# Neighbourhood attention with a stationary split V and a feature-major output, and later q/k weights split in the V stage

## The chip, the cores and the metric

One core of a Trainium2 chip runs the whole program. The metric is device time in microseconds, from runs of the complete kernel. The core has five instruction streams: TensorE (PE, matmuls, with its weight loads as PEld), VectorE (DVE), ScalarE (ACT), GpSimd (POOL) and SyncE (SP, which issues most of the loads). Each stream runs its instructions in order; they wait for each other by semaphores. SBUF is the working memory with 128 partitions, PSUM is where TensorE writes.

## The reference

One encoder layer in float32 over 1280 tokens (256 of a prompt, 1024 of a sample), model width 1024:

```
proj = rmsnorm(x) @ w_in            # columns: latents for group A | q, k, v for group B
a = mla_group(...)                  # 8 heads, dense attention over low-rank latents
b = na_group(...)                   # 8 heads of 64, 2-D neighbourhood attention
mix = concat(rmsnorm(a) * g_a, rmsnorm(b) * g_b)
x = x + mix @ w_o
x = x + (silu(h2 @ w_gate) * (h2 @ w_up)) @ w_down      # h2 = rmsnorm(x)
y = rmsnorm(x)
```

In group B each token attends to a window of at most 8 rows x 16 columns of a grid 64 wide, with a learned bias:

```
s = where(col_mask, q_row @ k_band.T + bias, -1e30)
p = softmax(s)
o = p @ v_band
```

## The kernel before

Tokens are reordered on the host so that a window falls into few tiles of 128 tokens: a query tile of the sample (tiles 2 to 9) needs its own key tile and its two neighbours, the two of the prompt (tiles 0 and 1) need each other. Products that must keep float32 accuracy are made in the type F32R: an operand is split into a high and a low part, and `mm3` (L108) issues three matmuls, high by high, high by low and low by high.

The stages follow each other. The first makes the normalised input, kept transposed as `hT_h` and `hT_l`, and the latents of group A. Then come q and k of the first pair of heads (`qk_weights`, L325, and `qk_ftile`, L336). `qk_weights` loads a raw 128-column weight, scales and splits it on GpSimd (L331, L333 through L94 and L96) into `wqk_h` and `wqk_l`, each with two buffers. `qk_ftile` projects it in three chunks of tokens into the PSUM tile `pj` and evicts it.

The V stage (L380 to L398) loads eight raw V weights into eight buffers, splits them on ScalarE and VectorE (`split_g`, L133), and for each of ten token tiles makes 24 matmuls into a bank of the two-bank PSUM tile `na_t`. One copy on ScalarE (L397) puts the result into `V`, in plain float32, which stays in SBUF for all heads.

The neighbourhood attention runs over four pairs of heads (L529). `na_bias(p)` (L414) loads and adds up the bias of the pair on GpSimd. `na_pair(p, ...)` (L455) takes ten query tiles, and in each of them two heads. For one head of one query tile:

- a copy of the query part on GpSimd (`qz`, L485), two score matmuls (L486, L487)
- bias and row extreme on VectorE (L497), exponential and row sum on ScalarE (L500)
- a transpose of each key tile's probabilities on TensorE (L504) into `na_t`, evicted by ScalarE for the first head (L507) and by VectorE for the second (L509)
- the product with V (L512): the transposed probabilities are stationary, 64 columns of `V` move, in plain float32. Each such call appears in the trace as two matmuls.

Then the query tile is divided by its row sums on VectorE (L517, L519) and stored token-major to `b_d`. While one pair attends, the projections of the next pair's q and k are what else TensorE has; the last pair has none, but some first projections of the latent attention (`project_first`, L665), held behind units of the last pair by `held`.

After the latent attention (L743) the output stage takes token tiles in turn. `mix_in` (L863) loads both groups' halves, makes their sums of squares and scales each half by its own factor on GpSimd (L877); `mix_T` (L882) transposes the eight 128-column blocks on TensorE and splits them; `out_proj` (L897) makes 24 matmuls for each half of the output into one PSUM bank and adds the residual on VectorE (L907). The FFN follows.

The order on SP's queue is the order of the program. On the other engines a planner orders the instructions at build time by its own estimate of their times, with earlier code preferred; `tc.issue_after(x)` puts an instruction behind `x` on its engine. A pool's tile with `bufs=n` has n slots: a new use of a slot waits until the former one is finished. Pools are stacked from both ends of SBUF, and a pool that is allocated where another was released waits tile by tile.

Of the kernel before, what the change touches and what calls it, by code (L numbers as in the profile page):

```python
# [11 lines left out]
F32 = mybir.dt.float32  # L12
# [6 lines left out]
P = 128  # L19
# [9 lines left out]
DH = 64  # L29
# [10 lines left out]
def encoder_trunk(ctx: ExitStack, tc: tile.TileContext, x_tm, x_T, g_attn, w_c, w_v, w_qk,  # L40
# [8 lines left out]
    b_d = tc.dram_tile([NTOK, 512], F32, name="b_d")  # L49
# [22 lines left out]
    def store_r(out, in_):  # L72
        nc.scalar.dma_start(out=out.bitcast(F32), in_=in_.bitcast(F32))

# [44 lines left out]
    rb = pool("rb", side="right")  # L119
    ra = pool("ra", side="right")  # L120
# [18 lines left out]
    def load_wc(kc):  # L139
        nm = {0: "wqk_raw", 1: "wqk_h", 2: "wqk_l", 3: "wqk_h", 4: "wqk_l", 7: "wqk_raw"}.get(kc)  # L140
        raw = (rb.tile([P, KC, P], F32, name=nm, bufs=1 if nm == "wqk_raw" else 2)
# [104 lines left out]
    def load_wr():  # L246
        raw = (rb.tile([P, KC, P], F32, name="wqk_raw").rearrange("p a b -> p (a b)")
               [:, 0:768].rearrange("p (c n) -> p c n", c=3))
        load(raw, w_qr)
        split_w(wr[:, 0], wr[:, 1], raw)  # L250
# [74 lines left out]
    def qk_weights(i):  # L325
        raw = rb.tile([P, KC, P], F32, name="wqk_raw")
        load(raw, w_qk[i])
        wh = rb.tile([P, KC, P], F32R, name="wqk_h", bufs=2)
        wl = rb.tile([P, KC, P], F32R, name="wqk_l", bufs=2)
        for ks in (slice(0, 4), slice(4, 8)):  # L330
            nc.gpsimd.tensor_tensor(out=raw[:, ks], in0=raw[:, ks], op=ALU.mult,  # L331
                                    in1=ga[:, ks].unsqueeze(2).to_broadcast([P, 4, P]))
            step["qkw"] = split_w(wh[:, ks], wl[:, ks], raw[:, ks])  # L333
        wqk[i] = wh, wl

    def qk_ftile(i, chunks=CHUNKS):  # L336
        wh, wl = wqk[i]
        dst = rq if (i // 2) % 2 == 0 else rc
        nm = "qk"[i % 2]
        if i not in qk:  # L340
            qk[i] = ([dst.tile([P, NTOK], F32R, name=f"{nm}{x}") for x in "ab"] +
                     [dst.tile([P, NTOK], F32R, name="kl") if nm == "k" else None])
        ab, kl = qk[i][0:2], qk[i][2]
# [32 lines left out]
    ra.release()  # L376
    pa.release()
# [3 lines left out]
    V = rV.tile([P, NT, 512], F32, name="V")  # L381
    rv = pool("rv", side="right")
    wv = []
    for kc in range(KC):
        raw = rv.tile([P, 512], F32, name="wv_raw", bufs=8)
        load(raw, w_v[kc])
        h = rv.tile([P, 512], F32R, name=f"wv_h{kc}")
        l = rv.tile([P, 512], F32R, name=f"wv_l{kc}")
        step["wv", kc] = split_g(h, l, raw, kc)
        wv.append((h, l))  # L390
    for t in range(NT):
        ts_ = slice(t * P, (t + 1) * P)
        pv = pb.tile([P, 512], F32, name="na_t", bufs=2)
        for kc in range(KC):
            mm3(pv, hT_h[:, kc, ts_], hT_l[:, kc, ts_], wv[kc][0], wv[kc][1],
                kc == 0, kc == KC - 1)
        nc.scalar.copy(out=V[:, t], in_=pv)  # L397
    rv.release()  # L398
    qk_ftile(1, CHUNKS[1:])


    rc = pool("rc", side="right")
    rcm = pool("rcm", side="right")
# [1054 lines left out]
```

## Time and profile before

| | |
|---|---|
| runs of the kernel | 1612.18, 1613.79, 1613.88 us (median 1613.79) |
| profiled execution, its span | 1610.3 us (the page gives no other time of it) |
| granted TensorE clock, mean | 0.998 |
| TensorE busy | 1582.5 us, 98% of the span |
| VectorE, ScalarE, GpSimd busy | 893.3, 717.2, 666.1 us |
| V stage | 137 to 193 us |
| neighbourhood attention | 193 to 381 us |
| latent attention | 381 to 663 us |
| output stage | 663 to 791 us |

The span is the time from the first to the last instruction on the profiled core. "Busy" is time in which an engine had an instruction running; matmuls overlap one another, so the duration of one matmul is longer than the step from its start to the next one's. An "x" is a count; `<-` in brackets names what ended the idle time before an instruction.

### The profile page before, as it was taken

How to read it: one execution, taken by the hardware profiler on the slowest of the kernel's cores; microseconds unless marked ns; L12 is line 12 of the kernel's file. 1: busy time of each engine (PE TensorE's matmuls, PEld its weight loads, DVE VectorE, ACT ScalarE, POOL GpSimd, SP SyncE). 2: the span in 40 equal slices, each digit the busy share in tenths (PEclk: the TensorE clock that was granted, in tenths of full speed). 3: DMA queues.
4: the chain of work that ended last, by engine and by line, in shares of the span. 5: the costliest groups of instructions: out<-in, count | busy, mean ns of one | idle time of the engine just before them, and what ended most of it. 6: DMA issues, size and time to landing. Idle time of an engine off the chain costs nothing.

```text
span 1610.3 us, 25767 instructions
## 1 busy us (share of the span) xinstructions
PE 1582.5 (98%) x9616; PEld 1443.1 (90%) x9616; DVE 893.3 (55%) x1501; ACT 717.2 (45%) x1492; POOL 666.1 (41%) x833
## 2 busy tenths in 40 slices
PE   8999999999999999999999999999999999999998
PEld 8998789998888888888899999999999998888886
DVE  5853045566677777443583444334444246886676
ACT  6533144465777777544453323233222332443334
POOL 4633235544211129224676665565666651010002
PEclk9999999999999999999999999999999999999999
DMA  8626022152100030234312232222232237843534
GB/s 294 202 70 160 19 53 63 37 209 62 32 20 26 24 119 20 80 118 144 125 67 65 89 110 97 71 87 89 97 110 76 70 128 269 296 140 96 157 103 155
DMA packets 121772, 171.09 MB, mean 106 GB/s; under 512 B 35376, under 2 KB 65840, under 8 KB 121648
## 3 DMA queue, kind: packets, MB, share of 16 engines
q1 hardware_dynamic: 78880, 120.30, 24.3%
q10 hardware_dynamic: 41952, 46.08, 8.2%
q0 software_dynamic: 816, 3.08, 0.5%
q8 instruction: 75, 1.23, 0.3%
q14 instruction: 49, 0.40, 0.1%
HBM read 118.96 MB, written 50.46 MB: 105 GB/s over the span
## 4 chain that ended last, share of the span: by engine, by line
PE 90%; POOL 3%; ACT 2%; DVE 2%; DMA 1%; issue 1%; SPq 0%; ACTq 0%; POOLq 0%; DVEq 0%
PE M L112 11%; PE M L110 10%; PE M L111 10%; PE d L111 5%; PE d L110 5%; PE d L112 5%; PE o L788 4%; PE tp L778 4%; PE na_o L512 3%; PE po L110 2%; PE pj L110 2%; PE pj L111 2%; PE pj L112 2%; PE po L111 2%; PE po L112 2%; PE S L110 2%
## 5 line engine op out<-in xcount | busy, mean ns | idle before, releaser
L111 PE MATMUL M<-S,wc 128*128 128x320 f32 x1056 | 323.8, 308 | 0.0
L110 PE MATMUL M<-S,wc 128*128 128x320 f32 x1056 | 321.3, 309 | 2.5 <-ACT S L962 1.2
L112 PE MATMUL M<-S,wc 128*128 128x320 f32 x1056 | 312.0, 309 | 2.4 <-POOL wc L970 2.4
L110 PEld LDWEIGHTS M<-S,wc 128*128 128x128 f32 x1056 | 197.3, 188 | 3.7 <-ACT S L962 1.5
L111 PEld LDWEIGHTS M<-S,wc 128*128 128x128 f32 x1056 | 198.2, 188 | 0.0
L112 PEld LDWEIGHTS M<-S,wc 128*128 128x128 f32 x1056 | 194.7, 188 | 3.0 <-POOL wc L970 3.0
L970 POOL TENSOR_TENSOR wc<-A,wc 128x512 fp32r<-128x512 f32 x86 | 121.1, 1409 | 81.6 <-ACT wc L969 81.5
L1052 DVE TENSOR_TENSOR z<-M,z 128x320 f32<-128x320 f32 x120 | 57.2, 487 | 129.6 <-PE M L112 109.1
L969 ACT CAST wc<-A 128x512 fp32r<-128x512 f32 x86 | 53.5, 622 | 158.4 <-PE M L111 148.8
L970 POOL TENSOR_TENSOR wc<-sum,wc 128x512 fp32r<-128x512 f32 x62 | 88.5, 1427 | 85.8 <-ACT wc L969 85.7
L1052 DVE TENSOR_TENSOR zB<-M,zB 128x320 f32<-128x320 f32 x100 | 47.6, 488 | 133.4 <-PE M L112 109.9
L111 PE MATMUL d<-S,S 128*128 128x512 f32 (+1 forms) x314 | 121.1, 386 | 0.0
L112 PE MATMUL d<-S,S 128*128 128x512 f32 (+1 forms) x314 | 120.7, 386 | 0.0
L110 PE MATMUL d<-S,S 128*128 128x512 f32 (+1 forms) x314 | 120.4, 387 | 0.0
L100 DVE TENSOR_TENSOR PT<-tp,PT 128x512 fp32r<-128x512 f32 (+1 forms) x144 | 93.2, 658 | 33.9 <-ACT PT L99 32.7
L969 ACT CAST wc<-sum 128x512 fp32r<-128x512 f32 x62 | 38.4, 619 | 144.0 <-PE M L111 99.6
L99 ACT CAST PT<-tp 128x512 fp32r<-128x512 f32 (+1 forms) x144 | 79.2, 567 | 33.5 <-PE tp L778 30.2
L770 DVE TENSOR_REDUCE mm<-S 128x1 f32<-128x1024 f32 (+1 forms) x80 | 85.0, 1062 | 13.5 <-PE S L112 11.9
L1099 ACT CAST S<-as 128x640 fp32r<-128x640 f32 x58 | 42.2, 728 | 105.7 <-issue 62.7
L772 ACT ACTIVATE ex<-S,mm 128x1024 f32<-128x1024 f32 (+1 forms) x80 | 79.7, 997 | 14.9 <-DVE mm L770 13.6
L801 POOL TENSOR_TENSOR ob<-ob 128x128 f32<-128x128 f32 x40 | 18.5, 461 | 160.8 <-ACT ob L798 157.3
L788 PE MATMUL o<-PT,v 128*128 128x256 f32 x544 | 80.4, 287 | 0.9 <-ACT PT L99 0.9
(432 smaller groups left out, 4115.8 us busy)
## 6 DMA issues: line engine op xcount, KB each, us to landing
as<-act_d SPq DMA_DIRECT2D x73, 320.0 KB
w<-in_w_down_dram SPq DMA_DIRECT2D x44, 256.0 KB
act_d<-z ACTq DMA_DIRECT2D x35, 320.0 KB
act_d<-zB ACTq DMA_DIRECT2D x35, 320.0 KB
A<-in_w_gate_dram SPq DMA_DIRECT2D x42, 256.0 KB
A<-in_w_up_dram SPq DMA_DIRECT2D x42, 256.0 KB
x<-in_x_tm_dram SPq DMA_DIRECT2D x20, 512.0 KB
cT_d<-stg ACTq DMA_DIRECT2D x20, 320.0 KB
```

The lines of the kernel that those rows point to most:

```text
L99: i = nc.scalar.copy(out=hi, in_=ps)
L100: nc.vector.tensor_sub(out=lo, in0=ps, in1=hi)
L110: nc.tensor.matmul(out, lhsT=sh, rhs=mh, start=first, stop=False, **kw)
L111: nc.tensor.matmul(out, lhsT=sh, rhs=ml, start=False, stop=False, **kw)
L112: return nc.tensor.matmul(out, lhsT=sl, rhs=mh, start=False, stop=last, **kw).ins
L770: nc.vector.reduce_max(out=nm[:, u:u + 1], in_=S, axis=AX.X, negate=True)
L772: nc.scalar.activation(ex, S, AF.Exp, bias=nm[:, u:u + 1], scale=1.0, accum_out=l[:, u:u + 1])
L778: nc.tensor.transpose(tp[:, j], ex[:, kt * P:(kt + 1) * P], ident)
L788: nc.tensor.matmul(oT, lhsT=vv, rhs=pt[s][g][:, j], start=kt == 0 and s == 0, stop=kt == nkt - 1 and s == 1)
L969: i0 = nc.scalar.copy(out=hi, in_=raw)
L970: i1 = nc.gpsimd.tensor_tensor(out=lo, in0=raw, in1=hi, op=ALU.subtract)
L1052: nc.vector.tensor_add(out=o, in0=ps, in1=a)
```

## The change

It touches five places.

1. **V.** The evicted V of each token tile is split into high and low parts, `[head][part][64]`, by ScalarE and VectorE (`split_ps`). The first pair's stays in SBUF, as five tiles of two token tiles each (`na_values`); the other three pairs' are stored to DRAM (`vn_d`) from GpSimd's queue and read back by SP, three tiles ahead of a pair and two within it (`bring`). The raw V weights have four buffers in place of eight.
2. **Product with V.** `na_pair` takes query tiles two at a time. Each head's exponentials are multiplied by the reciprocal of their sum on GpSimd before the transposes, the transposed tile is evicted as a high part by ScalarE and a low part by VectorE, and the product has the 128 columns of split V stationary. The moving operand is the high and then the low part of the probabilities: 256 columns for a key tile that both query tiles need, 128 for one that only one needs. The two 64-row halves of the result are added (one copy on ScalarE, one addition on VectorE for each head), and the result is stored feature-major to `bT_d`.
3. **Weights.** The q and k weights of pairs 1 to 3 are loaded, scaled and split in the V stage by ScalarE and VectorE (`later_weights`, twelve half-weights in four pieces each), stored to `wqk_d` from ScalarE's queue, and read back by SP as `wqk_h` and `wqk_l`. The split on GpSimd is left for pair 0 only. In program order, the weights of pairs 2 and 3 are fetched before the preceding pair attends.
4. **Bias.** A pair's sample bias is made after the pair before it, in one buffer (`na_bias`); the prompt's in two steps (`na_bias_p`). The forced order of the first pair's `qz` copies is dropped.
5. **Output stage.** Group B's half arrives feature-major and is split without a transpose or a scaling; its sum of squares is made by a square on ScalarE, two additions on GpSimd and a matmul with ones. Group A's half is transposed unscaled. `out_proj` keeps the two groups in two PSUM banks, and two `scalar_tensor_tensor` on VectorE scale and add them. The same 48 matmuls a tile remain.

`held` now names pair 3's first three double tiles in place of query tiles 0, 2, 5 and 7.

```diff
-    V = rV.tile([P, NT, 512], F32, name="V")
...
-        nc.scalar.copy(out=V[:, t], in_=pv)
+    VORD = ((2, 3), (4, 5), (6, 7), (8, 9), (0, 1))
+    def na_values(x, n, from_=None):
+        ts = VORD[n]
+        v = rV.tile([P, 2, 2, 2, DH], F32R, name="vn", bufs=8)
+        x.update({t: v[:, i] for i, t in enumerate(ts)})
+        if from_ is not None:
+            load_r(v.rearrange("p t h s d -> p t (h s d)"), from_[:, ts[0]:ts[0] + 2])
...
+    def later_weights(n):
+        i, ks = 2 + n // 2, slice(4 * (n % 2), 4 * (n % 2) + 4)
+        raw = rv.tile([P, 512], F32, name="wv_raw", bufs=4).rearrange("p (a b) -> p a b", b=P)
+        load(raw, w_qk[i, :, ks])
+        w = wst[n] if n < 2 else rv.tile([P, 2, 4, P], F32R, name="wst", bufs=2)
+        for c in range(4):
+            split_g(w[:, 0, c], w[:, 1, c], raw[:, c], ks.start + c)
+        store_r(wqk_d[i, :, :, ks].rearrange("s p c n -> p s c n"), w)
+    for n in range(4):
+        later_weights(n)
+    bs0 = na_bias(0, load_bias(0))
+    for n in range(4, 12):
+        later_weights(n)
...
+        split_ps(first_v[t][:, :, 0], first_v[t][:, :, 1], pv[:, 0:2])
+        v = vs[t] if t < 2 else rv.tile([P, HEADS - 2, 2, DH], F32R, name="vs", bufs=2)
+        split_ps(v[:, :, 0], v[:, :, 1], pv[:, 2:])
+        store_pr(vn_d[:, :, t].rearrange("q p f -> p q f"),
+                 v.rearrange("p (q h) s d -> p q (h s d)", h=2))
...
+        for d, pairs in enumerate([(2 * n, 2 * n + 1) for n in range(4)] + [None]):
+            qts = (0, 1) if pairs is None else tuple(2 + j for j in pairs)
+            wide = [[qts[0] - 1], [qts[1] + 1]]
+            wide = [[] if pairs is None or not 2 <= w[0] < NT else w for w in wide]
+            o = pb.tile([P, 2, 2 * P], F32, name="na_o", bufs=2)
+            pts = [rc.tile([P, 2, 3, 2, P], F32R, name="na_pt", bufs=2) for _ in range(2)]
+            for u in range(2):
+                qt = qts[u]
+                kts = list(qts) + wide[u]
...
+                    nc.vector.reciprocal(r[:, hh:hh + 1], l[:, hh:hh + 1])
+                    nc.gpsimd.tensor_scalar(out=sb, in0=sb, scalar1=r[:, hh:hh + 1], scalar2=1.0,
+                                            op0=ALU.mult, op1=ALU.mult)
+                    tp = pb.tile([P, 3, P], F32, name="na_t", bufs=2)[:, 0:len(kts)]
+                    for i, kt in enumerate(kts):
+                        a = (kt - k0) * P
+                        nc.tensor.transpose(tp[:, i], sb[:, a:a + P], ident)
+                    pt = pts[hh][:, :, 0:len(kts), u]
+                    split_ps(pt[:, 0], pt[:, 1], tp)
+                    if u == 0:
+                        continue
+                    jobs = [(kt, b, slice(0, 2)) for b, kt in enumerate(qts)]
+                    jobs += [(w[0], 2, slice(c, c + 1)) for c, w in enumerate(wide) if w]
+                    jobs = [(*job, x) for job in jobs for x in range(2)]
+                    for i, (kt, b, cs, x) in enumerate(jobs):
+                        step["na", p, d] = nc.tensor.matmul(
+                            o[:, hh, cs.start * P:cs.stop * P],
+                            lhsT=v[kt][:, hh].rearrange("p s d -> p (s d)"),
+                            rhs=pts[hh][:, x, b, cs].rearrange("p c q -> p (c q)"),
+                            start=i == 0, stop=i == len(jobs) - 1, skip_group_check=True).ins
+            for hh in range(2):
+                own, oth = slice(DH * hh, DH * hh + DH), slice(DH - DH * hh, 2 * DH - DH * hh)
+                nc.scalar.copy(out=tmp[own], in_=o[oth, hh])
+                nc.vector.tensor_add(out=ob[own], in0=o[own, hh], in1=tmp[own])
+            if d in (1, 2):
+                bring(d + 2)
+            (store_p if last else store)(bT_d[p, :, qts[0] * P:qts[0] * P + 2 * P], ob)
...
-        load(mx[:, 512:], b_d[ts_, :])
+        bt = mx[:, 512:].rearrange("p (c q) -> p c q", c=4)
+        load(bt, bT_d[:, :, ts_].rearrange("c p t -> p c t"))
+        nc.scalar.copy(out=mT[:, 0, 4:8], in_=bt)
+        nc.vector.tensor_sub(out=mT[:, 1, 4:8], in0=bt, in1=mT[:, 0, 4:8])
...
+        nc.tensor.matmul(ps, lhsT=sq[:, 512:512 + P], rhs=ones[:, 0:1], start=True, stop=True)
...
+                nc.vector.scalar_tensor_tensor(out=x[:, hs], in0=ps, scalar=r[:, n:n + 1],
+                                               in1=x[:, hs], op0=ALU.mult, op1=ALU.add)
```

More of the change, by code (lines that the diff above doesn't have):

```diff
@@ L420, in na_bias @@
             load(g[8 * qr:8 * qr + 8].rearrange("p r h j -> p (r h) j"), src)
[L421 to L429 removed]
+        if p == 0:
+            load(mi_s[:, 0], m_int)
+            load(mi_s[:, 1], m_edge)
+        return g
+    def na_bias(p, g):
+        bs = rce.tile([P, 2, 2, 384], F32, name="b_s")
+        bs = [bs[:, hh] for hh in range(2)]
         for hh in range(2):
```

312 lines of the change are left out of this document (148 added, 164 removed).

## The prediction

> **What bounds the kernel now.** I read the totals and the chain that ended last first, then the busy time in stretches cut at the borders of the stages, then the merged pieces of the chain for what one instruction of each kind occupies.
>
> ```profile
> span 1610.3 us, 25767 instructions
> ...
> PE 1582.5 (98%) x9616; PEld 1443.1 (90%) x9616; DVE 893.3 (55%) x1501; ACT 717.2 (45%) x1492; POOL 666.1 (41%) x833
> ...
> PE 90%; POOL 3%; ACT 2%; DVE 2%; DMA 1%; issue 1%; SPq 0%; ACTq 0%; POOLq 0%; DVEq 0%
> ```
>
> TensorE is busy for 98% of the span and is 90% of the chain. So an edit is worth what it takes off TensorE, as long as nothing else becomes the limit where it acts. The next view shows where that holds; its columns are the length of the stretch and the busy time of PE, PEld, DVE, ACT and POOL.
>
> ```profile
> core 0: us, PE busy (x) PEld busy (x) DVE busy (x) ACT busy (x) POOL busy (x), PEclk, DMA share, GB/s
> 137.00:193.00 56.00, 55.78 (x243) 45.15 (x242) 7.15 (x11) 12.11 (x21) 19.75 (x32) 1.00 0.25 56
> ...
> 193.00:254.00 61.00, 59.95 (x380) 53.06 (x378) 25.86 (x82) 27.53 (x72) 23.08 (x47) 1.00 0.20 43
> 254.00:305.00 51.00, 50.81 (x340) 46.22 (x339) 26.04 (x84) 25.80 (x71) 25.97 (x54) 1.00 0.25 54
> 305.00:337.00 32.00, 32.00 (x200) 28.72 (x199) 15.81 (x49) 15.52 (x43) 11.70 (x33) 1.00 0.15 32
> 337.00:381.00 44.00, 43.22 (x342) 40.63 (x341) 31.84 (x113) 29.20 (x83) 25.46 (x60) 1.00 0.64 219
> 381.00:663.00 282.00, 277.54 (x1804) 244.10 (x1803) 206.97 (x315) 207.41 (x440) 89.60 (x139) 1.00 0.14 42
> 663.00:791.00 128.00, 127.93 (x632) 104.09 (x631) 44.20 (x66) 47.34 (x116) 45.95 (x67) 1.00 0.36 121
> ```
>
> They are the V projection, the neighbourhood attention (193 to 381, the last 44 us of it without projections of q and k to fill), the latent attention and the output projection. TensorE is full in all of them. But VectorE is at 51% in the second stretch of the neighbourhood attention (26.04 of 51) and at 72% in the last (31.84 of 44), and the change gives it work there.
>
> **What one TensorE instruction occupies.** Merged pieces of the chain in order of time (start, us, what), and the forms of the instructions in them:
>
> ```profile
> 223.12 1.28 PE na_o L512 x12
> 224.40 0.66 PE na_t L504 x6
> 407.55 1.87 PE o L788 x16
> 1590.08 0.91 PE d L110 x4
> ...
> L512 PE MATMUL na_o<-V,na_pt 128*128 128x64 f32 x416 | 54.0, 269 | 1.3 <-DVE na_pt L509 0.7 <-ACT na_pt L507 0.5
> L504 PE MATMUL na_t<-ident,na_sb 128*128 128x128 f32 x208 | 33.1, 275 | 0.3 <-ACT na_sb L500 0.2
> ```
>
> The old product with V takes 1.28/12 = 0.107 us for 64 moving columns, and there are 416 of them, two for each of the 208 calls. A transpose takes 0.66/6 = 0.110 us for 128 columns. The latent attention's product with a stationary split V and 256 moving columns takes 1.87/16 = 0.117 us, and 512 columns take 0.91/4 = 0.228. So 64, 128 and 256 columns cost nearly the same here: each of these loads a full stationary tile.
>
> **The product with V.** Removed: 416 x 0.107 = 44.5 us. Added, for each head: five pairs of query tiles x 2 shared key tiles x 2 parts = 20 matmuls of 256 columns, and 6 outer key tiles x 2 parts = 12 of 128. For 8 heads that is 160 x 0.117 = 18.7 us and 96 at a price that no row has, since no F32R matmul moves 128 columns. From below it is half of the 256-column row, 0.058 us; from above four passes, which is a 512-column row, 0.228. I take 0.110, the transpose, because 64 and 128 columns cost the same above: 10.6 us. So 29.3 us replace 44.5: **-15.2 us of TensorE** (-3.9 from above, -20.2 from below).
>
> By the Trainium skill, TensorE: Matmul & The Clock Gate, section "Back-to-back issue gap", a lone matmul of 128 columns would be due every 56 ns, about 81 in a stream with weight loads. With 81 ns, an estimate from that page, the 96 would cost 7.8 us and the sum below would be about 2 us lower. The same page's section "LDWEIGHTS" has 128 stationary columns load in 107 ns, and with that figure the three rows here agree.
>
> **Where that saving counts.** Of the old products, this many records lie in each stretch (92, 104, 53, 170):
>
> ```profile
> 193.00:254.00 61.00, 11.91 (x92) 11.49 (x92) 2.31 (x8) 1.00 0.20 43
> 254.00:305.00 51.00, 13.00 (x104) 13.01 (x104) 2.92 (x10) 1.00 0.25 54
> 305.00:337.00 32.00, 6.32 (x53) 6.67 (x53) 1.46 (x5) 1.00 0.15 32
> 337.00:381.00 44.00, 22.75 (x170) 21.66 (x168) 4.88 (x17) 1.00 0.64 219
> ```
>
> Before 337 lie 249 of 419, or 59%, so 9.0 of the 15.2 us. After 337 nothing covers the other engines, so their new work is counted with these rows:
>
> ```profile
> L509 DVE COPY na_pt<-na_t 128x384 f32<-128x384 f32 x24 | 13.3, 556 | 6.1 <-PE na_t L504 5.7
> L507 ACT COPY na_pt<-na_t 128x384 f32<-128x384 f32 x24 | 11.4, 476 | 20.3 <-PE na_t L504 20.2
> L517 DVE RECIPROCAL na_r<-na_l 128x2 f32<-128x2 f32 x40 | 6.6, 165 | 9.3 <-ACT na_sb L500 9.0
> L519 DVE TENSOR_TENSOR na_b<-na_o,na_r 128x128 f32<-128x128 f32 x30 | 8.7, 290 | 30.7 <-PE na_o L512 30.1
> ...
> L792 ACT COPY os<-o 128x256 f32<-128x256 f32 x40 | 14.9, 373 | 13.3 <-PE o L788 13.0
> L877 POOL TENSOR_SCALAR m<-m,rm 128x512 f32<-128x512 f32 x16 | 10.9, 693 | 0.8
> ```
>
> Now each query tile has its probabilities evicted once by ScalarE and once by VectorE; after, each head's are evicted by both. VectorE gets per query tile one eviction (0.5 as a mean of the widths), one reciprocal (0.165) and one addition of 64x256 (0.4, as a 256-wide copy), and loses a 0.29: +0.78 us. ScalarE gets one eviction (0.43) and one copy (0.37): +0.8. The last stretch holds 170/10.4 = 16.3 query tiles, 10.4 matmuls each, so VectorE rises from 31.84 to 44.6 us and ScalarE from 29.2 to 42.2, in 44 us. There VectorE becomes the limit and TensorE's 6.2 us are lost: I put that stretch at 46 us, **+2** (0, if the planner moves query tiles forward under the projections; +6, if the engines reach only 90%). In the stretch from 254 VectorE rises by 7.8 to 34 of 47, which leaves TensorE the limit. That is the share that it has in the latent attention, 206.97 of 282, where TensorE stands idle for 4.46, or 1.6%. I charge that on the 135 us left there: **+2**.
>
> **Waits that are added.** A transpose now waits for exponential, reciprocal, the scaling on GpSimd (0.693 for 512 columns, so about 0.55 for 384) and only then runs. Behind the scaling on GpSimd stand the qz copies of the next heads, without which the second score matmul cannot start; behind the transpose on TensorE stand the projections. GpSimd has room: it takes over 80 scalings, some 36 us, and gives up the six later weights,
>
> ```profile
> 216.17 2.04 POOL L331 TENSOR_TENSOR wqk_raw<-wqk_raw,ga 128x512 f32<-128x512 f32 x2
> ...
> 218.99 1.20 POOL L94 TENSOR_SCALAR wqk_h<-wqk_raw 128x512 fp32r<-128x512 f32 x2
> ...
> 220.15 2.53 POOL L96 TENSOR_TENSOR wqk_l<-wqk_raw,wqk_h 128x512 fp32r<-128x512 f32 x2
> ```
>
> which are 6 x 5.8 = 35 us. On SP's queue the loads of weights 5 and 7 wait for the projection whose slots they take, and the next pair's bias and values stand behind; the projection is over by then, so I charge nothing. It would be one transfer of TensorE's cover, some 5 us a pair, if not.
>
> **V stage.** V's eviction becomes four instructions in place of one, the ten stores of V issue from GpSimd, and 48 pieces of weight are split by ScalarE and VectorE (about 0.25 and 0.29 each, rows below). That is 12 + 2 us for ScalarE and 14 + 8 for VectorE, plus twelve store issues (a third of a us) in ScalarE's queue, each waiting for VectorE's low half with V's evictions behind it. ScalarE is at 12.11 of 56 and VectorE at 7.15, and an eviction is due only every 5.49 us, with two banks, so TensorE's 55.78 hide it; uncovered it is some 16 us.
>
> ```profile
> 182.45 0.59 ACT L397 COPY V<-na_t 128x512 f32<-128x512 f32 x1 [4.91 <-PE na_t L112]
> 187.94 0.59 ACT L397 COPY V<-na_t 128x512 f32<-128x512 f32 x1 [4.91 <-PE na_t L112]
> ...
> 104.96 0.25 ACT L99 CAST stg<-trc 128x128 fp32r<-128x128 f32 x1
> 105.84 0.29 DVE L100 TENSOR_TENSOR stg<-trc,stg 128x128 fp32r<-128x128 f32 x1
> ...
> 137.33 4.06 DVE L135 SCALAR_TENSOR_TENSOR wv_l<-wv_raw,ga,wv_h 128x512 fp32r<-128x512 f32 x6
> ```
>
> The raw V weights get four buffers in place of eight, so the fifth's load waits for the first split, from 137.33; TensorE is full there and its first V tiles need all eight: **+1** (0 to 4).
>
> **Output stage.** Forty of the 80 transposes go (-4.4 us at 0.110); ten sums of squares by matmul come, two instructions each at 0.107 (+2.1): **-2.3**. The second addition per half is on VectorE, at 44.20 of 128.
>
> **Sum**, against the profiled execution's span of 1610.3, the only time that its page gives: -9.0 + 2 + 2 + 1 - 2.3 = -6.3 us. The runs lie 1.9 to 3.6 us above that span, the median 1613.8 at 3.5; from the median this makes 1607.5, and I forecast **1607**.
>
> **Rivals.**
> Full gain: the planner spreads the query tiles under the projections, so that the last stretch shrinks too: -15.2 - 2.3 + 1 = -16.5, **1597**. For it: VectorE has 25 of 51 us free from 254. Against it: pair 3's scores need the last projection.
> Dear narrow matmuls: 128 columns cost 0.228. Then TensorE saves 3.9, of which 2.3 before 337: -2.3 + 2 + 2 + 1 - 2.3 = +0.4, **1614**. For it: every F32R matmul of the trace moves at least 256 columns. Against it: the flat cost of 64 and 128.
> Slower, the longer chain uncovered: TensorE takes its instructions in order, and where a transpose stands ready in the plan but waits for the scaling, nothing passes it. Where attention runs bare today a wait looks like this:
>
> ```profile
> 194.15 0.44 PE L486 MATMUL na_s<-ka,qa 128*128 128x384 f32 x1 [0.52 <-DVE na_m L497]
> ...
> 195.75 0.66 PE L512 MATMUL na_o<-V,na_pt 128*128 128x64 f32 x4 [0.46 <-ACT na_pt L507]
> ```
>
> About 0.5 us. It decides from 6.3/0.5 = 13 of the 80 heads of query tiles; with half of them it costs 20, **1628**. Against it: the planner places the projections between, and today such waits are few.
>
> **Chances.** Forecast 45% (1602 to 1611), full gain 17%, dear narrow matmuls 15%, slower chain 23%. What a measurement of this kernel tells from no change is 0.2%, 3.2 us. Faster: 0.17 and nearly all of the 0.45, 0.59. Within: 0.15 and a little of it, 0.17. Slower: 0.24. The range goes from a full gain with the cheap price to the slower chain: 1594 to 1626.
>
> **What would show it.** The 128-column F32R matmuls follow each other by about 0.11 us; the product with V occupies about 29 us; the stretches before the last pair shorten by some 9 us with TensorE full; in the last, VectorE is above 90% and TensorE idles; a V tile still comes every 5.5 us; the output stage loses 2. Wrong it is if transposes wait for GpSimd all along, or if the last pair shrinks as well.

## The result and the profile after

The changed kernel takes 1630.8 us (median; 1629.5 to 1633.2) beside 1613.0 (1611.9 to 1613.9) of the kernel before on the same chip: a ratio of 1.011, 95% interval 1.0098 to 1.0122. It is slower by some 18 us, where 6 were to be gained, and lies above the range.

The totals of its profiled execution:

```profile
span 1627.7 us, 26067 instructions
...
PE 1580.4 (97%) x9436; PEld 1433.2 (88%) x9436; DVE 960.6 (59%) x1679; ACT 763.5 (47%) x1620; POOL 685.6 (42%) x888
...
PE 51%; POOL 2%; issue 1%; DVE 1%; ACT 0%; DMA 0%; POOLq 0%; SPq 0%; ACTq 0%; DVEq 0%
```

TensorE has 180 instructions fewer and is busy for 2 us less, but the span is 17.4 longer. The shares of the chain add up to little more than half: it could be followed back only to 734 us, so it says nothing on the attention, and the stretches have to. The same stretches as before the change, with the same columns (length, then busy time of PE, PEld, DVE, ACT and POOL, granted clock, DMA share):

```profile
137.00:193.00 56.00, 53.35 (x229) 43.09 (x228) 28.27 (x71) 27.17 (x75) 12.08 (x21) 0.97 0.82 272
193.00:254.00 61.00, 58.54 (x330) 50.60 (x328) 35.12 (x119) 36.67 (x101) 30.84 (x74) 0.94 0.38 98
254.00:305.00 51.00, 49.11 (x302) 42.27 (x301) 31.60 (x103) 33.07 (x89) 24.72 (x61) 1.00 0.37 103
305.00:337.00 32.00, 31.72 (x200) 28.13 (x199) 20.64 (x65) 19.93 (x54) 12.21 (x30) 1.00 0.42 119
337.00:381.00 44.00, 35.98 (x196) 29.56 (x195) 25.93 (x86) 27.54 (x73) 35.16 (x80) 0.92 0.63 217
```

TensorE is no longer full, and the granted clock, 1.00 in all of these rows before, is down to 0.94 and 0.92. VectorE is far from full: 25.93 of 44 in the last row.

The borders of the stages tell where the time went. V's last matmul starts at 199.5 us (193.0 before), the last product of the neighbourhood attention ends at 399.1 (380.5), the program at 1627.7 (1610.3). So the V stage costs 6.5 us, the attention 12.1, and all behind it gains 1.2. (Twelve projections of q and k, some 1.4 us, moved from the attention into the V stage, so the first number is high and the second low by that much.) The attention alone, from border to border, of the kernel before and then of the changed one:

```profile
193.20:380.50 187.30, 185.27 (x1252) 168.04 (x1251) 99.13 (x324) 97.97 (x265) 86.20 (x191) 1.00 0.31 86
```

```profile
199.70:399.10 199.40, 183.25 (x1083) 156.89 (x1081) 125.44 (x407) 128.84 (x346) 109.20 (x255) 0.97 0.40 119
```

I add up, for each kind of TensorE instruction in these two stretches, the time from its start to the next start. The product with V goes from 44.3 to 35.3 us; idle time goes from 2.0 to 16.3, the scores from 29.3 to 32.8, the transposes from 20.4 to 22.8, 1.2 us more of the latent attention's scores lie inside, and the projections take 0.3 less. That makes the 12.1, to 0.2. Scores and transposes are the same instructions as before; they take longer behind waits and at a lower clock.

**What a wait does.** The first V evictions. ScalarE's rows, then TensorE's (start, duration, instruction, and in brackets how long it stood idle and for what):

```profile
146.84 2.16 ACT L140 ACTIVATE wst<-wv_raw,ga 128x128 fp32r<-128x128 f32 x7
148.87 0.37 ACTq L75 DMA_DIRECT2D wqk_d<-wst  x1
148.90 0.39 ACT L140 ACTIVATE wst<-wv_raw,ga 128x128 fp32r<-128x128 f32 x1
149.92 0.37 ACTq L75 DMA_DIRECT2D wqk_d<-wst  x1
150.33 0.43 ACT L104 CAST vn<-na_t 128x128 fp32r<-128x128 f32 x2 [1.04 <-DVE wst L141]
...
149.13 0.39 PE L116 MATMUL na_t<-wv_l,hT_h 128*128 128x512 f32 x1
149.36 0.40 PE L117 MATMUL na_t<-wv_h,hT_l 128*128 128x512 f32 x1
152.17 0.51 PE L115 MATMUL na_t<-wv_h,hT_h 128*128 128x512 f32 x1 [2.41 <-DVE vs L105]
152.48 0.63 PE L116 MATMUL na_t<-wv_l,hT_h 128*128 128x512 f32 x1
152.91 0.63 PE L117 MATMUL na_t<-wv_h,hT_l 128*128 128x512 f32 x1
```

Eight pieces of the later weights and two store issues stand on ScalarE ahead of V's first eviction, so both banks stay full and TensorE waits 2.41 us. Behind the wait the same matmul takes 0.63 in place of 0.39, for 3.3 us, and each step 0.43 in place of 0.23.

The end of the first pair, GpSimd's rows and then TensorE's:

```profile
239.16 5.00 POOL L448 TENSOR_TENSOR b_s<-g_s,mi_s 128x128 f32<-128x128 f32 x12 [0.15 <-issue]
244.23 0.29 POOL L532 CAST qz<-qb 64x128 fp32r<-64x128 f32 x1
244.62 0.94 POOL L550 TENSOR_SCALAR na_sb<-na_sb,na_r 128x256 f32<-128x256 f32 x2
...
243.63 0.28 PE L534 MATMUL na_s<-kl,qz 128*128 128x256 f32 x1
245.15 1.15 PE L555 MATMUL na_t<-ident,na_sb 128*128 128x128 f32 x4 [1.25 <-POOL na_sb L550]
246.30 0.58 PE L564 MATMUL na_o<-na_pt,vn 128*128 128x256 f32 x1
246.68 0.41 PE L533 MATMUL na_s<-ka,qa 128*128 128x256 f32 x1
```

Twelve additions for the next pair's bias, 5 us, stand on GpSimd ahead of the scaling, and the transposes behind it wait. The product's matmul that follows takes 0.58 in place of 0.28, and TensorE stays at that pace until about 251. No projection covers this: they run from 199.7 to 236.6 and again from 255.7, once the next weights are there.

The granted clock in the trace shows what happened. It is 0.5 in four stretches from the V stage to the end of the attention, 152.5 to 155.9, 244.6 to 251.5, 357.3 to 360.7 and 374.3 to 377.7 us, each of them 3.41 us long or twice that. Here is the second of them with the 3.41 us ahead of it, and then another stretch of that length with a wait in it (columns as above):

```profile
241.22:244.63 3.41, 2.18 (x15) 1.53 (x13) 3.08 (x11) 2.84 (x9) 3.25 (x10) 1.00 0.26 77
244.63:251.45 6.82, 6.29 (x27) 5.63 (x28) 3.36 (x16) 3.56 (x11) 5.93 (x15) 0.50 0.16 41
...
350.44:353.85 3.41, 2.21 (x14) 1.47 (x12) 2.72 (x10) 3.15 (x10) 3.13 (x11) 1.00 1.01 422
```

In the 3.41 us ahead of the four, TensorE was busy for 1.00, 2.18, 0.87 and 1.71 us. Behind the last row, with 2.21, the clock stayed full. So in this trace the half clock follows stretches of 3.41 us with little work in them, and near 2.2 us of work it went either way. The length of a single wait doesn't tell it: of the 1.25 us before 245.15 only 0.72 lie in the first row, beside shorter waits.

**The last pair runs bare.** From the last projection to the last product, the transposes alone, of the kernel before and of the changed one (length, busy time and count on PE and PEld, clock):

```profile
337.00:380.50 43.50, 13.87 (x79) 9.85 (x79) 1.00 0.65 222
```

```profile
347.00:399.10 52.10, 11.36 (x64) 7.53 (x64) 0.93 0.54 190
```

Before, 79 recorded transposes took 43.5 us, after 64 take 52.1: with 2.6 transposes a head (208 for 80), 1.43 us a head became 2.1.

### The profile page after: what moved, and what is told of

It is laid out like the page before. It is cut to its first block, busy times and chain, and to the rows that moved or that the text cites. A ratio compares the mean times of both kernels' runs of the same rounds, so it can differ in the third digit from the quotient of the medians.

```text
span 1627.7 us, 26067 instructions
## 1 busy us (share of the span) xinstructions
PE 1580.4 (97%) x9436; PEld 1433.2 (88%) x9436; DVE 960.6 (59%) x1679; ACT 763.5 (47%) x1620; POOL 685.6 (42%) x888
## 4 chain that ended last, share of the span: by engine, by line
PE 51%; POOL 2%; issue 1%; DVE 1%; ACT 0%; DMA 0%; POOLq 0%; SPq 0%; ACTq 0%; DVEq 0%
PE M L117 11%; PE M L115 11%; PE M L116 11%; PE d L115 5%; PE d L116 5%; PE d L117 5%; POOL wc L1033 1%; POOL sum L1043 0%; PE po L117 0%; PE po L115 0%; PE po L116 0%; POOL S L1043 0%; PE trh L989 0%; DMA A<-in_w_down_dram 0%; POOL A L1011 0%
## 5 line engine op out<-in xcount | busy, mean ns | idle before, releaser
L833 DVE TENSOR_REDUCE mm<-S 128x1 f32<-128x1024 f32 (+1 forms) x80 | 84.9, 1061 | 12.1 <-PE S L117 10.3
L841 PE MATMUL tp<-ident,ex 128*128 128x128 f32 x544 | 79.1, 274 | 2.5 <-DVE PT L105 1.4
```

Of the source, the lines that this page charges most:

```text
L833: nc.vector.reduce_max(out=nm[:, u:u + 1], in_=S, axis=AX.X, negate=True)
L841: nc.tensor.transpose(tp[:, j], ex[:, kt * P:(kt + 1) * P], ident)
```

## The experiments

Three theories at first: A, the projections that fill TensorE come late; B, the scaling on GpSimd sets the pace; C, the V stage. Behind each time stand its ratio to runs of the kernel before on the same chip and the 95% interval of that ratio.

**The weights' loads earlier in the queue.**

```diff
-        bp = na_bias_p(p, gp, None if more else load_gp(p, 1))
         if more:
             for i in range(2 if p else 0):
                 qk_weights(2 * p + 2 + i)
+        bp = na_bias_p(p, gp, None if more else load_gp(p, 1))
+        if more:
```

> The changed kernel, with the loads of the next pair's split q and k weights put ahead of that pair's prompt bias on the load queue. In the profile of the changed kernel the projections stand still from 236.6 to 255.7 us and from 296.1 to 305.6, while the weights' loads stand in the queue behind a load that waits for GpSimd. Theory A (the fill is late): the projections resume some 8 us earlier in each of the two gaps, TensorE's 4.6 us of idle time there and the low clock behind it (about 3 us) go, 1623 to 1626. Theory B (the scaling on GpSimd in the softmax chain sets the loss): the bare stretch at the end only gets longer by what the fill is used up earlier, within 3 us of 1631. Theory C (the V stage): no change, 1631.

1648.4 us (1.0218, 1.0202 to 1.0233): 17.5 us slower still. The load queue in this run, and then its stretch behind the last projection:

```profile
245.06 0.43 SPq L81 DMA_DIRECT2D wqk_l<-wqk_d  x1
...
262.34 35.63 SPq L81 DMA_DIRECT2D vn<-vn_d  x5
298.32 0.32 SPq L81 DMA_DIRECT2D wqk_h<-wqk_d  x1
```

```profile
348.00:413.80 65.80, 48.90 (x272) 39.70 (x270) 43.93 (x145) 41.80 (x117) 45.96 (x103) 0.90 0.51 166
```

The second pair of weights came 7.6 us earlier (its first load at 243.6 against 251.2) and its projections were used up by 286.7; the last weights still stood behind the values' loads until 298.3. The last projection comes no earlier than before, and more of the attention is left behind it: 76 recorded transposes in place of 64, in 65.8 us in place of 52.1. So A falls, in its sign. I read it so that the earlier load spends the fill earlier, and that the fill is worth most where it is spread.

**The V stage.**

```diff
-    for n in range(4):
-        later_weights(n)
     bs0 = na_bias(0, load_bias(0))
-    for n in range(4, 12):
-        later_weights(n)
     for t in range(NT):
...
+        for n in range(12 * t // 10, 12 * (t + 1) // 10):
+            later_weights(n)
```

> The changed kernel, with the split of the later q and k weights issued in pieces behind the V tiles in place of ahead of them, so that V's evictions no longer stand behind 8 pieces of weight on ScalarE and VectorE. Theory C (the V stage costs 4.4 us: 2.6 us of TensorE idle at 149.6 us, and 1.8 us at half clock behind it): 1625 to 1628. Theory A and B: the later weights come some us later and all else stays, 1630 to 1632.

1630.8 us (1.0117, 1.01 to 1.0134). V's last matmul comes 2.8 us earlier, at 196.7, but the attention ends at 400.5. What is gained ahead of the attention is lost in it. So its price was measured on the kernel before, where TensorE is full. The early split alone, with the changed kernel's `later_weights` and four raw buffers (theory F in what was expected: the later weights come late and are projected in one block; theory D comes with the evictions below):

```diff
+    for n in range(12):
+        later_weights(n)
     for t in range(NT):
...
+        if i >= 2:
+            load_r(wh, wqk_d[i, 0])
+            load_r(wl, wqk_d[i, 1])
```

> The kernel before the change with one part of it alone: the later q and k weights are split in the V stage by ScalarE and VectorE, stored, and loaded ready, and the raw V weights have four buffers; attention, values and output stage are as before. Theory F (late weights, and projections that come in a dense block once their weights are ready): slower by 4 to 10 us, 1618 to 1624. Theory D: the V stage may lose its 3 us of idle time, the rest stays, 1612 to 1617.

1616.1 us (1.0023, 1.0013 to 1.0033): +3.6. And with each piece behind a V tile, by the same edit as above:

> The kernel before the change with the later q and k weights split early by ScalarE and VectorE, as in the earlier run (1616.1), and each piece behind a V tile in place of all ahead of them. If the stall of the V tiles behind the pieces is what the early split costs: 1612 to 1614. If it is the weights that are ready at once and so projected in one block: 1615 to 1618.

1614.0 beside 1614.4 of the kernel before (0.9997, 0.9988 to 1.0006). So the early split by itself costs nothing that the interval shows; the order of ScalarE's and VectorE's queues costs the 3.6 us.

**The scaling.** Taken out of the changed kernel (the GpSimd instruction goes and nothing takes its place), and then put on VectorE:

```diff
-                    nc.gpsimd.tensor_scalar(out=sb, in0=sb, scalar1=r[:, hh:hh + 1], scalar2=1.0,
+                    nc.vector.tensor_scalar(out=sb, in0=sb, scalar1=r[:, hh:hh + 1], scalar2=1.0,
```

> The changed kernel without the scaling of the probabilities on GpSimd (this leaves out the normalisation). Theory B (the transposes wait for GpSimd, whose bias additions, memsets and weight splits stand ahead of the scaling; after 347 us the attention runs bare for 52 us against 44 before): the bare stretch falls back toward 44 us and the waits at 244 and 354 us go, 1616 to 1622. Theory A: only a hop of 0.6 us per head goes, which the projections cover where there are any, 1627 to 1630.

> The changed kernel with the scaling of the probabilities on VectorE in place of GpSimd, right behind the reciprocal, which is there as well. Theory B (what stands ahead of the scaling on GpSimd, and the hop to it): nearly as far down as with no scaling, 1617 to 1624. If the length of the chain alone counts: the scaling is about as long on VectorE (0.3 to 0.5 us), which is then the busiest engine in the bare stretch (25.9 of 44 us now, some 33 with the scaling), 1626 to 1632.

1626.2 (1.008, 1.0061 to 1.01) and 1625.1 us (1.0074, 1.0059 to 1.0089): 4.6 and 5.7 less than the changed kernel. B was to bring 9 to 15; both runs lie between the ranges of their theories. With the scaling on VectorE, the last stretch reads

```profile
337.00:381.00 44.00, 39.04 (x232) 33.17 (x231) 39.19 (x128) 32.56 (x88) 28.75 (x66) 0.92 0.63 220
```

where VectorE, at 39.19 of 44, is now the busiest engine, and the run with no scaling at all is no faster. So something else held the pace as well. Theory D: the second eviction.

**One eviction a head.** The high half only, as in the old kernel from one engine; the matmuls stay, reading it twice.

```diff
-                    split_ps(pt[:, 0], pt[:, 1], tp)
+                    if hh == 0:
+                        nc.scalar.copy(out=pt[:, 0], in_=tp)
+                    else:
+                        nc.vector.tensor_copy(out=pt[:, 0], in_=tp)
...
-                            rhs=pts[hh][:, x, b, cs].rearrange("p c q -> p (c q)"),
+                            rhs=pts[hh][:, 0, b, cs].rearrange("p c q -> p (c q)"),
```

> The changed kernel with each head's probabilities evicted once, by ScalarE for one head and VectorE for the other as before the change; the product reads the high half in both of its matmuls, so TensorE's instructions stay the same (this leaves out the low half of the probabilities). Theory D (two evictions in series for each head, by both engines, set the pace where the attention runs bare: 2.07 us a head from the last projection on, 1.43 before the change): the bare stretch comes near the old pace, 25 heads x 0.6 = 15 us, and the gaps at 240 and 300 us lose some, 1610 to 1618. Theory E (only one pair of query tiles has buffers for its probabilities): less work, but the same order of waits, 1622 to 1628. Theory F (the weights loaded late and the fill used up early): 1626 to 1631.

And in the space of the low half:

```diff
-            pts = [rc.tile([P, 2, 3, 2, P], F32R, name="na_pt", bufs=2) for _ in range(2)]
+            pts = [rc.tile([P, 1, 3, 2, P], F32R, name="na_pt", bufs=4) for _ in range(2)]
```

> As the run with the high half only, with the space of the unused low half given to twice the buffers of probabilities, two pairs of query tiles in place of one (this leaves out the low half). Theory E: another 4 to 10 us below the run with the high half only. Theory D: within 2 us of it.

1630.9 (1.0117, 1.0101 to 1.0132) and 1632.3 us (1.0118, 1.0101 to 1.0135): nothing, and no gain from buffers (E falls). Theory D by itself misses too: only the range of theory F, late weights, holds the first of them. But without the scaling too (the first run's edit and the scaling's two lines taken out):

> As the run with the high half only, and without the scaling on GpSimd too (this leaves out the low half and the normalisation). Theory D: both are gone that the change adds to the chain of a head, so what is left is the saving on TensorE: 1597 to 1606, the full gain of the prediction. Theory F: the weights are as late as before, 1618 to 1626.

1612.6 us (1.0000, 0.9991 to 1.0009): 18.2 less than the changed kernel, though not the 1597 to 1606 of theory D, nor the 1618 to 1626 of theory F. Its attention:

```profile
199.60:379.80 180.20, 171.71 (x1077) 151.69 (x1075) 107.62 (x365) 112.62 (x304) 66.53 (x174) 0.99 0.45 129
```

180.2 us, 7.1 below the kernel before; the product's starts add up to 30.1, with 1.7 of it at half clock. So the new product saves about what was forecast when neither addition is there, and the two additions cost it 19.2 (199.4 - 180.2). The program as a whole gains nothing, because the V stage still ends 6.4 us late (199.4).

**A store in ScalarE's queue.** In the run with one eviction ScalarE stood 4.6 us at a store in the last stretch; in the changed kernel 3 us:

```profile
353.54 0.36 ACT L573 COPY na_h<-na_o 64x256 f32<-64x256 f32 x1
356.50 0.33 ACTq L69 DMA_DIRECT2D bT_d<-na_b  x1
356.87 0.65 ACT L104 CAST na_pt<-na_t 128x256 fp32r<-128x256 f32 x2 [2.97 <-DMA cT<-cT_d]
...
357.30 0.58 PE L564 MATMUL na_o<-na_pt,vn 128*128 128x256 f32 x1 [1.77 <-ACT na_pt L104]
```

```diff
-            (store_p if last else store)(bT_d[p, :, qts[0] * P:qts[0] * P + 2 * P], ob)
+            (store_p if last or (p == PAIRS - 2 and d >= 3) else store)(bT_d[p, :, qts[0] * P:qts[0] * P + 2 * P], ob)
```

> The changed kernel with the last two stores of the third pair issued by GpSimd in place of ScalarE (before the change the prompt tiles' store of that pair went there). In the profile of the changed kernel ScalarE stands from 353.9 to 356.5 us at such a store while the transfers of the next stage are under way, with evictions behind it, and TensorE then runs at half clock to 360. Theory G (this stall and the low clock behind it are a good part of the loss): 1622 to 1627. Theory H (the bare stretch is paced by the chain through GpSimd and by the two evictions, so that the time comes back at the next wait): 1628 to 1632.

> The high half only, evicted once (this leaves out the low half of the probabilities), with the store of the run before. Theory G (the stall of 4.6 us at that store, and half clock for 10 us, hid what the single eviction saves): 1616 to 1624. Theory H (with the scaling on GpSimd in the chain, fewer evictions gain nothing): 1626 to 1631.

With everything else as changed: 1630.6 us (1.0104, 1.0089 to 1.0119), nothing, as theory H has it. With one eviction: 1625.3 (1.0073, 1.0058 to 1.0088), 5.6 below the same run without the edit, and just below the range of theory H, not in that of G. So the stall had hidden what one eviction saves, about 5.3 (1630.6 - 1625.3), but it is not what the changed kernel loses.

**Each addition on the kernel before.** The scaling between exponential and transposes; an eviction by ScalarE and then VectorE; both.

```diff
+                nc.vector.reciprocal(r[:, hh:hh + 1], l[:, hh:hh + 1])
+                nc.gpsimd.tensor_scalar(out=sb, in0=sb, scalar1=r[:, hh:hh + 1], scalar2=1.0,
+                                        op0=ALU.mult, op1=ALU.mult)
...
+                nc.scalar.copy(out=pt, in_=tp)
+                nc.vector.tensor_tensor(out=pt, in0=tp, in1=pt, op=ALU.max)
```

> The kernel before the change with one of its additions alone: the probabilities are scaled on GpSimd between the exponential and the transposes, two reciprocals of one column in place of one of two, and the product's eviction is a plain copy. If the longer chain costs by itself: 1620 to 1628, with waits of TensorE for GpSimd in the bare stretch. If TensorE's old product (1.43 us a head) covers it: 1612 to 1616.

> The kernel before the change with the other addition alone: each head's probabilities are evicted by ScalarE and then, from the same bank, by VectorE (which takes the larger of the bank and the copy, so the values stay the same), and the product waits for both. If the second eviction costs by itself: some 12 us more of VectorE in the bare stretch of 44 us, which then is its limit, 1616 to 1624. If TensorE's old product covers it: 1612 to 1615.

> The kernel before the change with the early scaling and the double eviction together, so the softmax chain of the changed kernel with the old product. Theory H (the bare pace is set by whichever of the two is left, so that neither alone moves it much when taken away): most of the cost comes with the first of them, and both together are within 4 us of the dearer one. If their costs add: the sum of the two runs' losses, 1624 to 1635.

1626.4 (1.0084, 1.0067 to 1.0101), 1618.8 (1.0043, 1.0028 to 1.0058) and 1632.2 us (1.0122, 1.0107 to 1.0137): +13.8, +6.1 and +19.6. Within their intervals they add (13.8 + 6.1 = 19.9), and both together lie 5.8 above the dearer one. Theory H as it is put here allowed 4; each interval is some 2.5 us to either side, so it is unlikely rather than excluded. The attention of the first and the third:

```profile
194.00:397.70 203.70, 194.68 (x1258) 175.09 (x1257) 105.67 (x366) 98.20 (x265) 140.91 (x287) 0.96 0.29 82
```

```profile
193.20:401.60 208.40, 196.08 (x1252) 174.00 (x1250) 118.78 (x405) 113.39 (x305) 140.77 (x287) 0.96 0.29 80
```

No engine but TensorE is above 70% busy. What TensorE waited for, in the first, is little, and GpSimd leads:

```profile
PE na_t L508 <- POOL na_sb L504: 3.6, 2, 2.3
PE na_o L516 <- DVE na_pt L513: 1.8, 4, 0.7
PE na_s L487 <- DVE na_m L498: 1.8, 4, 0.7
```

Of the 16.4 us by which its attention is longer than 187.3 (this profiled execution took 1629.2, 2.8 above the median), idle time is 7.0 (9.0 against 2.0); the rest is TensorE busy 9.4 us longer. The clock is 0.5 from 199.0 to 205.8 and from 349.2 to 359.4, and matmuls whose steps add up to 15.0 us start there, so some 7.5 of the 9.4 are the clock; 1.5 more are six matmuls of the latent attention that now lie inside.

**Towards a faster version.** The normalisation out of the chain, done on the reciprocal sums in the output stage; and that with one matmul in place of two:

```diff
+        nc.vector.reciprocal(lall, lall)
+        nc.tensor.transpose(tp, lall, ident)
...
+        nc.vector.tensor_mul(out=bt, in0=bt, in1=rb_)
         nc.scalar.copy(out=mT[:, 0, 4:8], in_=bt)
```

> The changed kernel with the whole computation: the probabilities are split without scaling, the reciprocal sums are transposed once a pair, stored, and multiplied in the output stage; later weights behind the V tiles, store on GpSimd. If the gains add up (4.6 of the scaling, 2.8 at the V stage's end, the reciprocals' 11 us of VectorE's queue): 1614 to 1621. If the two evictions alone still set the bare pace: 1622 to 1627.

> As the run normalised in the output stage, with the high half only, evicted once, and one matmul in place of two (this leaves out the low half of the probabilities): TensorE's product with V falls from 29 us to about 15. From 1612.6 without scaling and low half, another 14.5 us of TensorE go, of which about 60% lie where it is full, and 3 us at the V stage: 1598 to 1606. If the bare stretch keeps its 1.64 us a head for engines' work and all of the 14.5 us lie in waits: 1606 to 1612.

1689.0 (1.0464, 1.0447 to 1.0482) and 1674.7 us (1.0376, 1.0356 to 1.0396). The attention ends at 390.1 and 374.8, 9.0 and 24.3 before the changed kernel's; but both times lie far above what was expected. I had put the loaded reciprocals in the tile of the squares, and the sums of squares then came late: in each run TensorE waits 34.2 us for them in the output stage, and in the second the clock is at half for 55 us between 692 and 843. With the normalisation at the end of each pair instead, and then with seven small output buffers in place of one:

```diff
+        store_p(r_d[p].rearrange("t a q -> (t a) q"), rT)
...
+                ob, t = obs[d]
+                nc.gpsimd.tensor_tensor(out=ob, in0=ob, in1=rbc[:, 2 * x * P:2 * x * P + 2 * P], op=ALU.mult)
+                store_p(bT_d[p, :, t * P:t * P + 2 * P], ob)
```

> The changed kernel with neither addition: the high half only, evicted once, one matmul in place of two (this leaves out the low half of the probabilities), and the normalisation behind the product: the reciprocal sums of a pair are transposed once, stored, loaded across the partitions and multiplied by GpSimd into the pair's output before its store; later weights behind the V tiles, output stage as in the changed kernel. The run with one product ended the attention at 374.8 us, 5.7 before the old kernel's end of it, and lost its time in the output stage: 1600 to 1610. If the last pair's normalisation behind the attention delays the latent attention: 1610 to 1620.

> As the run with one product that is normalised per pair (it leaves out the low half of the probabilities), with seven buffers of 256 columns for the output in place of one of the whole pair, each multiplied and stored by itself. In that run TensorE stood 16.8 us in the last pair, until the pair before had been stored, with half clock behind it. If this one buffer was the whole of its excess: 1600 to 1607. If GpSimd's queue, which now issues three times as many transfers, delays the bias or the scores' operands: 1608 to 1618.

1625.8 (1.0086, 1.0071 to 1.0101) and 1619.5 us (1.0027, 1.0018 to 1.0037). The one buffer shows in the first as

```profile
PE na_o L563 <- DVE na_b L573: 17.2, 2, 16.8
```

and is down to one wait of 2.6 us in the second, whose attention ends at 376.6, 3.9 before that of the kernel before. Its time is lost behind it: from there to the end it takes 1241.7 us, against 1229.8. The clock is at half from 373.9 to 387.5 there, and TensorE stands idle for 2.6 us at 379; by my estimate (half of the 8.3 us of work at half clock behind the attention, and the wait) that is some 7 of these 11.9 us, and the rest was not followed. Both runs lie above all that was expected of them. No version here is faster than the kernel before.

## Why the prediction was wrong

**The step that failed is "Waits that are added".** It gave the longer chain no term in the sum, because GpSimd "has room" and because the projections lie between. GpSimd's room was there (109.20 of 199.4 us busy). But its other work comes in blocks, 5 us of bias additions at 239, and the scaling stands behind them; and the projections run out, at 236.6 and at 346.6. On the kernel before, the scaling alone costs 13.8 us and the second eviction 6.1; the prediction has the second eviction only as load of VectorE and ScalarE, and not as a wait. The rival "slower, the longer chain uncovered" had this mechanism, with 1628 us at 23%. Its price was too simple: it counted waits of 0.5 us, while with the scaling alone 7.0 of 16.4 us are idle time and some 7.5 the half clock that goes with it. That its 1628 comes near the measured 1630.8 is in part luck, since 6.5 us of the loss lie in the V stage, which it left at 1.

**The product with V** was priced rightly. The row of 15 matmuls, and what follows it:

```profile
231.53 1.84 PE L564 MATMUL na_o<-na_pt,vn 128*128 128x256 f32 x15
233.20 0.84 PE L555 MATMUL na_t<-ident,na_sb 128*128 128x128 f32 x6
```

15 starts in 1.67 us. Seven move 256 columns and eight 128: 7 x 0.117 leaves 0.106 for the narrow one, where 0.110 was taken. The sum, forecast at 29.3, is 30.1 in the run without the additions, of which 0.8 is the half clock; in the changed kernel, behind waits, it is 35.3. The rival of dear narrow matmuls is out. The estimate of 81 ns from the Trainium skill, TensorE: Matmul & The Clock Gate, section "Back-to-back issue gap", is not borne out; the transpose's row was the better guide.

**Where that saving counts.** Forecast were -9.0 with 2 and 2 off, -5. The changed kernel takes 147.3 us from the V stage to the end of the last projection (143.8 before) and 52.1 behind it (43.5 before). Without the additions the attention has -7.1, near the forecast, but not divided as it was: -4.9 ahead of the last projection's end (138.9 against 143.8, of which some 1.4 are the projections that moved into the V stage) and -2.2 behind it (41.3 against 43.5).

**The last stretch** was to cost 2, with VectorE as the limit at 44.6 of 44. VectorE was at 25.93. No engine fills the bare stretch (TensorE, the busiest, is at 40.58 of 52.10), so I take it to be paced by the chain, at 2.1 us a head, and the +6 that was kept for engines at 90% was no bound on that. The 2 us for idle time before it were a share of another stage (1.6%), with more work in flight; TensorE stood still for 4.6 us between the V stage and the last projection.

**V stage**: forecast 1 (0 to 4) and hidden; 6.5 in the profile, 3.6 alone on the kernel before. TensorE waited for no raw weight: its first V matmul starts at 138.6 (137.5 before, and 0.7 of that was there ahead of the stage), and its waits in the stage, 2.7 us, are for evictions. ScalarE stood 1.9 us for raw weights ahead of the pieces; what that adds to the late evictions was not tried. "Uncovered it is some 16" named the work, with a piece at 0.25 us on ScalarE where 0.39 was measured, but the cover was read as a sum over the stage, 12 and 7 of 56 us busy, where the first eviction of all stands behind eight pieces.

**The SP queue** was charged nothing, because the projection would be over by then. In the changed kernel the loads of the later weights start at 251.2 and 301.8, and the projections stand still from 236.6 to 255.7 and from 296.1 to 305.6 (before, the one pause of over 3 us is from 300.9 to 305.4). The 5 us a pair that were named as the stake are not what this costs: the run that loads earlier became slower, so the price of these two gaps stays open.

**Output stage**: -2.3 forecast. The stage's stretch before and after, of the kernel before and then of the changed one:

```profile
660.00:792.00 132.00, 131.93 (x656) 107.71 (x657) 47.37 (x71) 50.16 (x124) 47.53 (x70) 1.00 0.36 120
```

```profile
678.00:810.00 132.00, 129.37 (x640) 106.68 (x639) 67.61 (x100) 50.22 (x118) 54.73 (x76) 1.00 0.35 119
```

TensorE does 2.6 us less. From border to border, first transpose to last product, the stage is as long as before (132.7 against 132.8): the saved work became idle time, 2.2 us of it in waits for VectorE, which has more to do (67.61 in place of 47.37).

**What stays open.** The two additions cost 19.6 on the kernel before and 19.2 in the changed kernel's attention. But taken alone out of the changed kernel the scaling gives 4.6, against 13.8 when added alone. Stalls at ScalarE's stores (2.7 us in that run) may hide a part, as they hid the single eviction's; this was not tried. Product (35.3 against 29.3), scores (3.6) and transposes (2.4) exceed the forecast and their steps before by 12.0 us. Matmuls of these kinds whose steps add up to 12.8 us start at half clock, so 6.4 of it is the clock; why the other 5.6 are lost at full clock, a pipeline that empties in front of waits perhaps, is not shown. And without both additions TensorE still stands idle for 7.3 us behind the last projection (0.8 before); whether the pairing of query tiles or the new output additions cause that was not tried.

## What to carry to other kernels

An instruction that is added to a chain is hidden only while there is other work for the bound engine to do; look for where this fill ends, and price the chain there, per item, and not by waits. Ask what else the new link's engine has queued in blocks at that place, and whether moving the fill earlier only uses it up. A stage's busy share says nothing on its first instruction: the order in the queue does.

## What was not expected of the hardware

TensorE's clock falls to half behind short waits. By the Trainium skill, TensorE: Matmul & The Clock Gate, section "Part 1: The HAM clock gate", the clock returns to half after an idle window of about 3.4 us. Here shorter waits were followed by it: one wait of 2.41 us at 149.8 (0.63 for 0.39 behind it), one of 1.25 us at 243.9 with shorter gaps of 0.2 to 0.3 us ahead, and the wait of 1.77 us before 357.30 (0.58 for 0.28), where the 3.41 us ahead were still busy for 1.00, 2.18 and 0.87 us. The measurement decides. Not every wait has it: the clock stayed full behind one of 0.90 us at 352.0. At half clock 3.41 us lose some 1.7 and 6.82 us some 3.4, whatever the length of the wait itself, and this even where TensorE is 97% busy in the whole.

A store that an engine issues holds back all that is queued behind it: ScalarE stood 2.97 us at the store of 356.50, which the profile puts down to a load of another stage (`cT`).
